# An eight-core encoder block: a fixed program with barriers against a list-scheduled one over pooled buffers

## The chip, the cores and the metric

The kernel runs on all eight cores of one Trainium2 chip, as two dies of four cores. Each core computes four whole sequences and shares nothing with the others. The metric is the device time of the slowest core, in microseconds (us).

Executions come in two states. In the slow one, the cores of one die (sometimes of both) show a lower mean granted TensorE clock, and the time is some per cent longer. Every comparison below is between fast executions, unless it says otherwise. "Excess" below means time in which TensorE was not doing columns at its full pace; how it is counted is told with the result.

## The reference, cut to what matters

One layer of an encoder block, on x of 32 x 2048 x 1024, memory of 32 x 256 x 1024:

```python
h = rms_norm(x, norm1_g)
proj = h @ w_in                       # 1024 -> 9728
y_dil = dilated_mixture_attention(...)   # 8 heads of 64, three (window, dilation): (128,1) (512,4) (2048,16)
y_ret = bidirectional_retention(...)     # 4 heads, forward and backward scan, per-head norm, silu gate
y_mem = memory_cross_attention(...)      # 4 heads of 128 into 256 memory tokens
gates = sigmoid(gate_p).reshape(b, s, 3, d)
merged = gates[:,:,0]*(y_dil @ w_branch_dil) + gates[:,:,1]*(y_ret @ w_branch_ret) + gates[:,:,2]*(y_mem @ w_branch_mem)
x = x + merged @ w_out
h2 = rms_norm(x, norm2_g)
x = x + conv_glu_ffn(h2, ...)            # 1024 -> 2 x 2816, conv of width 3, gelu * gate, -> 1024
```

In dilated attention the queries and keys have a norm per head, the scores get a position bias and a band mask, and the three dilations are merged by their softmax denominators.

## The kernel before

It is an in-order program. Each operation names keys that it reads and writes, each engine gets its operations in program order, and a barrier stands after the first norm, retention, memory attention, dilated attention and the output projection. PSUM banks go round by number, and scratch buffers are fixed.

```python
    def barrier(self, engines=("tensor", "vector", "scalar", "sync")):
        lasts = set(self.last[e] for e in engines if self.last[e] is not None)
        lasts |= set(v for k, v in self.last_dma.items() if isinstance(k, str) and k.startswith("xa"))
        for e in engines:
            self.bar[e] |= lasts
    # ... (cut)
        def bank():
            i = cnt["bank"] % 8
            cnt["bank"] += 1
            return ps[i], "ps%d" % i
    # ... (cut)
        def wload(src_ap, ncols, view=None):            # f32 in DRAM, cast to bf16 by the GpSimd DMA, every sequence
            s = nxt("w", 3)
            dst = wbuf[s][:, 0:8 * ncols].rearrange("p (k n) -> p k n", k=8)
            pairs = src_ap if isinstance(src_ap, list) else [(src_ap, view)]
            for sa, vw in pairs:
                P.op("gpsimd", lambda e, sa=sa, vw=vw: e.dma_start(out=dst if vw is None else vw(dst), in_=sa),
                     writes=["wbuf%d" % s], dma="wbuf%d" % s)
            return dst, "wbuf%d" % s
```

Dilated attention is twelve units: four pairs of heads by three dilations. For a unit, `prep` makes projections and head norms, `attn` makes scores, exponentials, the product with the position weights, and the product with the values. The program interleaves the attention of one unit with the projections of the next, by hand:

```python
            for u, (c, g) in enumerate(cgs):
                other = None
                if u + 1 < len(cgs):
                    c2, g2 = cgs[u + 1]
                    w_, wk_c = prep_begin(c2, g2, (u + 1) % 2)
                    other = prep_gen(c2, g2, (u + 1) % 2, w_, wk_c)
                # ... (cut)
                    interleave([attn_gen(c, g, u % 2)] + ([other] if other is not None else []))
            # ... (cut)
            P.barrier()
```

## Time and profile before

| | before |
|---|---|
| median of the first 6 runs | 7391.37 us |
| fast runs | 7197.74 to 7277.08 us, most of them under 7216 |
| slow runs | up to 7952.08 us |
| one sequence in the profiled run | 1791 us (1876 to 3667) |
| DMA | 357.63 MB in 470,679 packets |

The profiled run of before was a fast one (7205.49 us). The lines of the profile that matter are in the prediction. To read the stage windows there: the length of a window less the time that its matmuls need at full pace is what a better order could win.

### The profile page before, as it was taken

To read this page: it belongs to the slowest core of one execution; us is meant where nothing else is said; L and a number is where in the kernel's file an instruction comes from. 1 tells how busy PE (TensorE), PEld (TensorE's weight loads), DVE (VectorE), ACT (ScalarE), POOL (GpSimd) and SP (SyncE) were. 2 spreads that over 40 slices of the span, in tenths; PEclk is the share of its full clock that TensorE was granted. 3 is DMA by queue.
4 is the path that set the end of the run, shared out by engine and by line. 5 is a ranking of instruction groups with operands and counts; after the bars stand their busy time and mean duration, and the time that the engine had idled before them with its cause. 6 is when DMAs were issued, how large, how long until landed. Compare 5 with 4: busy or idle time off the path is not lost.

```text
span 7203.9 us, 101543 instructions; the slowest of 8 cores (7167.4 to 7203.9 us)
## 1 busy us (share of the span) xinstructions
PE 5903.6 (82%) x34768; PEld 2937.8 (41%) x34768; DVE 3232.9 (45%) x4627; ACT 2848.7 (40%) x5072; POOL 350.9 (5%) x401
## 2 busy tenths in 40 slices
PE   6478889899647888989964788898996478889898
PEld 3134544344323554444432345444443234544444
DVE  4335544561343554456143355445614335544561
ACT  4466632220346663232034666322203466632330
POOL 0000010000000001000000000100000000010000
PEclk9598889999859888999975988899997598889999
DMA  3111241435211114143521112424352111242424
GB/s 79 22 15 19 26 47 36 101 42 111 71 25 17 19 21 53 36 101 41 117 77 15 16 19 26 48 41 96 42 115 80 15 15 19 26 48 46 94 39 113
DMA packets 470679, 357.63 MB, mean 50 GB/s; under 512 B 259616, under 2 KB 405408, under 8 KB 470176
## 3 DMA queue, kind: packets, MB, share of 16 engines
q0 software_dynamic: 403792, 178.41, 20.7%
q1 hardware_dynamic: 66384, 172.72, 7.5%
q8 instruction: 290, 4.75, 0.3%
q14 instruction: 213, 1.74, 0.1%
HBM read 462.36 MB, written 67.11 MB: 73 GB/s over the span
## 4 chain that ended last, share of the span: by engine, by line
PE 72%; DVE 9%; ACT 8%; DMA 6%; issue 5%; DVEq 0%; SPq 0%; ACTq 0%; POOLq 0%
PE ps L415 29%; PE ps L727 10%; PE ps L1091 7%; PE ps L760 5%; PE ps L990 5%; PE ps L869 2%; PE ps L648 2%; PE ps L496 2%; PE ps L836 1%; PE ps L736 1%; DMA out<-arena 1%; DMA wbuf<-w_out 1%; PE ps L1026 1%; DMA arena<-w_in 1%; PE ps L841 1%
## 5 line engine op out<-in xcount | busy, mean ns | idle before, releaser
L415 PE MATMUL ps<-hT,wbuf 128*128 128x512 bf16 x6656 | 1454.3, 382 | 19.6 <-DVE arena L1043 6.4
L415 PEld LDWEIGHTS ps<-hT,wbuf 128*128 128x128 bf16 x6656 | 654.7, 98 | 817.5 <-issue 43.6
L727 PE MATMUL ps<-hT,wbuf 128*128 128x512 bf16 x3072 | 784.3, 402 | 31.6 <-DVE arena L741 13.1
L415 PE MATMUL ps<-hT,arena 128*128 128x512 bf16 x3072 | 732.9, 382 | 67.4 <-DMA arena<-w_in 67.4
L760 PE MATMUL ps<-wbuf,hT 128*128 128x128 bf16 x6144 | 406.9, 229 | 133.9 <-DVE arena L741 133.9
L415 PEld LDWEIGHTS ps<-hT,arena 128*128 128x128 bf16 x3072 | 301.7, 98 | 434.9 <-issue 76.9
L760 PEld LDWEIGHTS ps<-wbuf,hT 128*128 128x128 bf16 x6144 | 393.4, 124 | 138.9 <-issue 136.0
L727 PEld LDWEIGHTS ps<-hT,wbuf 128*128 128x128 bf16 x3072 | 289.3, 102 | 379.8 <-issue 125.1
L853 DVE TENSOR_TENSOR arena<-arena 128x512 bf16<-128x512 bf16 (+2 forms) x672 | 238.8, 357 | 360.0 <-ACT arena L850 295.0
L990 PE MATMUL ps<-arena,wbuf 128*128 128x512 bf16 x1536 | 396.7, 381 | 0.0
L1063 ACT ACTIVATE arena<-arena 128x2048 f32<-128x2048 f32 x88 | 168.2, 1912 | 547.1 <-DVE arena L1061 547.1
L850 ACT ACTIVATE arena<-ps 128x512 bf16<-128x512 f32 (+2 forms) x672 | 325.6, 490 | 100.4 <-PE ps L841 42.8
L985 ACT ACTIVATE t_1<-ps 128x512 f32<-128x512 f32 x256 | 152.9, 597 | 504.7 <-PE ps L415 481.9
L1066 DVE TENSOR_TENSOR arena<-arena,ps 128x512 bf16<-128x512 f32 x352 | 242.2, 688 | 230.5 <-PE ps L415 154.2
L1091 PE MATMUL ps<-wbuf,arena 128*128 128x512 bf16 x1408 | 313.4, 386 | 22.7 <-DVE arena L1066 22.7
L730 ACT ACTIVATE tball<-ps 128x512 bf16<-128x512 f32 x384 | 229.4, 597 | 250.0 <-PE ps L727 244.2
L1053 ACT COPY arena<-ps 128x512 f32<-128x512 f32 x352 | 205.2, 583 | 308.1 <-PE ps L415 307.5
L741 DVE SCALAR_TENSOR_TENSOR arena<-ps,par,t_0 128x512 bf16<-128x512 f32 x192 | 190.8, 994 | 295.8 <-PE ps L727 149.4
L1091 PE MATMUL ps<-arena 128*128 128x512 bf16 x1408 | 307.0, 380 | 9.6 <-DVE t_0 L1100 6.8
L869 PE MATMUL ps<-arena 128*128 128x128 bf16 x2048 | 247.0, 234 | 80.1 <-DVE arena L853 29.9
L386 ACT ACTIVATE xs<-arena 128x1024 bf16<-128x1024 f32 x48 | 50.7, 1057 | 641.6 <-DMA arena<-x 575.3
L575 PE MATMUL ps<-tball,arena 128*128 128x128 bf16 x256 | 73.2, 286 | 256.3 <-DVE tball L566 256.3
(206 smaller groups left out, 8135.2 us busy)
## 6 DMA issues: line engine op xcount, KB each, us to landing
arena<-x SPq DMA_DIRECT2D x96, 512.0 KB, 6.1
wbuf<-w_ffn_in POOLq DMA_DIRECT2D x88, 512.0 KB, 6.2
wbuf<-w_in POOLq DMA_DIRECT2D x144, 256.0 KB, 4.5
arena<-w_in POOLq DMA_DIRECT2D x96, 256.0 KB, 4.6
wbuf<-w_in POOLq DMA_DIRECT2D x16, 1024.0 KB, 14.4
xt<-x SPq DMA_DIRECT2D x32, 512.0 KB, 4.5
out<-xt SPq DMA_DIRECT2D x32, 512.0 KB, 5.5
out<-arena SPq DMA_DIRECT2D x32, 512.0 KB, 5.2
```

The source lines that it names most:

```text
L415: P.op("tensor", lambda e, kc=kc: e.matmul(bk[:, 0:n], lhsT=w[:, kc, coff:coff + 128], rhs=rhsT[:, kc, t0:t0 + n], start=(kc == 0), stop=( ...
L727: P.op("tensor", lambda e, kc=kc: e.matmul(bk[:, 0:512], lhsT=w[:, kc, coff:coff + 128], rhs=hT[:, kc, tt * 512:(tt + 1) * 512], start=(kc ...
L730: P.op("scalar", lambda e: e.activation(out=sq[:], in_=bk[:, 0:512], func=AF.Square), reads=[bkey], writes=[sqk])
L741: P.op("vector", lambda e: e.scalar_tensor_tensor(out=outv, in0=bk[:, 0:512].rearrange("p (i c) -> p c i", c=r), scalar=par[:, gcol:gcol + 1],
L760: P.op("tensor", lambda e, kc=kc, li=li, t0=t0: e.matmul(vb[:, li * 128:(li + 1) * 128], lhsT=hT[:, kc, t0:t0 + r * 127 + 1:r], rhs=w[:, k ...
L850: P.op("scalar", lambda e, lo=lo, hi=hi: e.activation(out=praw[:, lo:hi], in_=bs[:, lo:hi], func=AF.Exp, scale=0.125), reads=[bsk], writes ...
L853: P.op(meng, lambda e, lo=lo, hi=hi: e.tensor_tensor(out=pT[:, lo:hi], in0=praw[:, lo:hi], in1=Ets[st_][hh][:, lo:hi], op=ALU.mult), reads ...
L869: P.op("tensor", lambda e, oc=oc, m=m, pcx=pcx, ix=ix, n=len(tl): e.matmul(bn[:, oc], lhsT=dv[:, cl * ntile + m, vsl], rhs=pT[:, pcx:pcx + ...
L990: P.op("tensor", lambda e, kc=kc, bp=bp, bi=bi, oc=oc, yb=yb, tsl=tsl: e.matmul(bp[:, 0:512], lhsT=wbr[bi][0][:, kc, oc * 128:(oc + 1) * 1 ...
L1053: P.op("scalar", lambda e, bu=bu, tt=tt: e.copy(out=ubuf[:, 1 + tt * 512:1 + (tt + 1) * 512], in_=bu[:, 0:512]), reads=[buk], writes=["ubuf"])
L1066: P.op("vector", lambda e, bg=bg, tt=tt, j=j: e.tensor_tensor(out=yT[:, j, tt * 512:(tt + 1) * 512], in0=cbuf[:, tt * 512:(tt + 1) * 512], ...
L1091: P.op("tensor", lambda e, bk=bks[tl][0], j=j, t=t: e.matmul(bk[:, 0:512], lhsT=yT[:, j, t * 128:(t + 1) * 128], rhs=w[:, j - j0, 0:512], ...
```

## The change

The intent is to let stages overlap. The whole program is written down as a graph, without barriers; buffers are taken from pools; and a list scheduler, run when the kernel is built, fixes the order on each engine from a cost per operation. Besides that: the feed-forward part works on half a sequence, so that it can begin earlier; the f32 weights are cast once and kept in DRAM as bf16 copies; the mean of retention's head norm is folded into centred value weights; Sigmoid becomes Tanh, Silu is built from Exp and Ln; row norms take their reciprocal roots on GpSimd.

The files are nearly wholly rewritten, so the diff is cut to its core (cuts are marked by dots; the remarks behind # are added here).

```diff
-    def barrier(self, engines=("tensor", "vector", "scalar", "sync")):
-        lasts = set(self.last[e] for e in engines if self.last[e] is not None)
-        ...
+class Pool:
+    def __init__(self, name, aps, reserve, psum=False):
+        self.name, self.aps, self.reserve, self.psum = name, aps, reserve, psum
+        ...
+    def mm(self, out, lhsT, rhs, start=True, stop=True, skip=False):
+        n = elems(proto(rhs))
+        c = max(n / 2.4 + 2.5, 26)
+        ...
+    def schedule(self):
+        ...
+        def fits(i):                                   # may operation i take the buffers it needs now?
+            ...
+                old = tls[0].seq == p.oldest
+                if not old and k - len(tls) < p.reserve:
+                    return p
+                for tl in tls:
+                    if tl.cap and not old and p.held.get(tl.cap[0], 0) >= tl.cap[1]:
+                        return p
+        ...
+                while future[e] and future[e][0][0] <= free[e]:
+                    r, i = heapq.heappop(future[e])
+                    heapq.heappush(avail[e], (ops[i]["prio"], i))      # of the ready ones, program order wins
-        ps = [ctx.enter_context(nc.psum_tensor("ps%d" % i, [128, 512], F32)) for i in range(8)]
+        psp = P.pool("ps", [... 8 banks ...], psum_reserve, psum=True)   # reserve 2
+        fp = P.pool("F", bufs("fb", 6, [128, 512], F32), 3)
+        bp = P.pool("B", bufs("bb", 12, [128, 512], BF16), 4)
+        wp = P.pool("W", bufs("wb", 10, [128, 8, 128], BF16), 3)
+        def load(dst, src, cache, key, sem, after=None):
+            if key in cached:
+                P.dma("sync", dst, cache, sem, ...)                    # bf16 copy
+            else:
+                P.dma("gpsimd", dst, src, sem, ...)                    # f32, cast
+                    P.dma("sync", cache, dst, ...)                     # write the copy
+                    cached.add(key)
+        def phase_d():
+            ...
+            dil_prep(0, 0, 0)
+            for u, (c, g) in enumerate(units):
+                dil_attn(c, g, u % 2)
+                if g == 2:
+                    dil_tail(c)
+                if u + 1 < len(units):
+                    dil_prep(units[u + 1][0], units[u + 1][1], (u + 1) % 2)
+        for b in range(nseq):
+            ret_pair(0)
+            ret_pair(1)
+            phase_m(b)
+            phase_d()
+            gates(0)
+            load_wout()
+            out_proj(b, 0)
+            gates(1)
+            out_proj(b, 1)
+            ffn_in(0)
+            ffn_out(b, 0)
+            ffn_in(1)
+            mark = len(P.ops)
+            ffn_out(b, 1)
+            if b + 1 < nseq:
+                P.shift = mark - len(P.ops)                            # next norm at the last FFN out's priority
+                phase_a(b + 1)
+                P.shift = 0
```

The attention of a unit is in the new kernel:

```python
            def score(tiles):
                bs = [new(psp), new(psp)]                              # one PSUM bank for each head of the pair
                # ... 64-row score matmuls of both heads, alternately
                for hh in range(2):
                    raw, p = new(bp)[:, 0:o], new(bp)[:, 0:o]
                    P.act(raw, bs[hh][:, 0:o], AF.Exp, scale=0.125)
                    # ... P.tt(p, raw, E, ALU.mult): product with exp(-slope * distance), zero outside the band
```

## The prediction

> **What bounds the kernel now.** I read in this order: the times and the cores (all eight cores lie between 7167.4 and 7203.9 us, granted clock 0.886 to 0.890, so the profile is an undisturbed one and no core stands out); the page; then one sequence cut into its stages; then what ended TensorE's waits. The page first:
>
> ```profile
> PE 5903.6 (82%) x34768; PEld 2937.8 (41%) x34768; DVE 3232.9 (45%) x4627; ACT 2848.7 (40%) x5072; POOL 350.9 (5%) x401
> ...
> PE   6478889899647888989964788898996478889898
> ...
> PEclk9598889999859888999975988899997598889999
> ```
>
> Each core does four sequences, one after the other; the pattern of ten slices repeats four times. TensorE is the busiest engine, VectorE and ScalarE are under half. In every sequence there is a hole where PE is 4 to 7 tenths busy and its clock falls to 5 to 7 tenths. The stage windows of the second sequence (columns: window, length, busy PE, PEld, DVE, ACT, POOL, then granted clock, DMA share, GB/s):
>
> ```profile
> 1876.00:2123.00 247.00, 162.88 (x928) 78.95 (x928) 93.77 (x193) 100.89 (x206) 2.62 (x3) 0.71 0.08 13
> 2123.00:2252.00 129.00, 79.50 (x308) 31.21 (x308) 28.84 (x42) 74.51 (x134) 6.99 (x8) 0.84 0.20 25
> 2252.00:2708.00 456.00, 388.79 (x3299) 231.17 (x3299) 237.25 (x409) 291.12 (x519) 25.97 (x30) 0.89 0.20 22
> 2708.00:2762.00 54.00, 47.04 (x382) 28.15 (x381) 34.26 (x63) 30.76 (x60) 0.74 (x1) 0.78 0.13 21
> 2762.00:3026.00 264.00, 248.93 (x1143) 112.40 (x1144) 113.33 (x162) 64.09 (x102) 21.85 (x25) 0.96 0.27 29
> 3026.00:3134.00 108.00, 70.93 (x395) 32.87 (x392) 53.49 (x69) 28.23 (x66) 5.60 (x6) 0.92 0.73 182
> 3134.00:3445.00 311.00, 305.36 (x1408) 137.99 (x1408) 193.95 (x155) 92.66 (x111) 17.43 (x20) 0.99 0.30 41
> 3445.00:3600.00 155.00, 154.84 (x704) 69.45 (x704) 18.57 (x27) 0.00 (x0) 5.20 (x6) 0.98 0.56 132
> 3600.00:3667.00 67.00, 16.37 (x130) 12.54 (x130) 33.72 (x37) 27.52 (x65) 0.00 (x0) 0.53 0.49 167
> ```
>
> They are: retention, memory attention, dilated attention (two windows), gates, output projection with its norm, FFN in, FFN out, and the first norm of the next sequence. Only FFN in and out are full (1408 matmuls in 311 us). Dilated attention, the longest, is bound by nothing in full: PE 436 us busy of 510, by modelled ends, ACT 322.
>
> How much of "busy" is work? The timeline inside FFN in gives the pace:
>
> ```profile
> 3199.72 10.52 PE L415 MATMUL ps<-hT,wbuf 128*128 128x512 bf16 x48
> ```
>
> Less one latency (380 ns), 47 steps take 10.14 us: **215.7 ns for a 512-column matmul**, 0.421 ns a column, at clock 0.99. In dilated attention 32 matmuls of 128 columns take 1.95 us, less 0.23 for the last: 55.5 ns each, 0.434 a column. So PE's real work can be counted in columns. What ends PE's waits, over the whole run:
>
> ```profile
> PE ps L575 <- DVE tball L566: 256.3, 32, 10.1
> PE ps L399 <- DVE xs L391: 211.0, 63, 35.0
> PE ps L760 <- DVE arena L741: 133.9, 12, 11.5
> PE ps L399 <- DVE tball L391: 93.3, 64, 5.8
> ...
> PE ps L415 <- DMA arena<-w_in: 67.4, 4, 18.7
> ...
> PE ps L1026 <- DMA wbuf<-w_out: 42.6, 8, 8.9
> ```
>
> These are chains at the start or inside of a stage (retention's per-head norm, the norms before transposes, the change from one attention unit to the next) with no other stage's work to put in, and weight loads asked for only after a barrier. The kernel is TensorE work plus these holes and cold clock.
>
> **What the Trainium skill says.** (1) "TensorE: Matmul & The Clock Gate", Part 1: the array's clock is halved after an idle window of about 3.4 us and comes back after a busy one. The trace agrees: 0.53 and 0.71 in the windows with PE idle, 0.99 in FFN in. (2) The same page and part: with three cores of a die dense, the die is held at 13/16 of the clock. This profile does not show it: all eight cores have 0.99 in FFN in. But four of the six runs of before took 7374.86 to 7594.88 us against 7197.74, which may be this. (3) Same page, "Back-to-back issue gap": 215.7 ns is the isolated figure for 512 columns, and a sustained 131 ns is given too. The trace has 215.7 and never 131, so I use 215.7. (4) "DMA: Bandwidth & Descriptors", "Issuing engines are not separate DMA queues": queues of all issuers share the same 16 DMA engines, so moving loads from GpSimd to SyncE buys issue time, not bandwidth.
>
> **The change part by part.**
>
> *TensorE's work hardly changes.* Columns of a sequence, after: input projection 76 chunks of 128 outputs plus 2 for keys projected twice, each 8 x 2048 = 16384: 1,277,952; FFN in 44 x 16384 = 720,896; FFN out 360,448; branch projections 196,608; output 131,072; attention scores and values (31 tiles, 28 and 16 per head, 8 heads, twice) 153,600; memory keys and values 16,384, its attention 49,152; head norms 58,368; retention 57,344; transposes 34,816. Sum 3,056,640. Before it is about 12,000 more (the mean matmul of retention, now folded into centred weights, and padded edge tiles): 0.4%. About 0.41 M of them are in 128-column matmuls. So 2.65 M x 0.421 + 0.41 M x 0.434 = 1116 + 178 = **1294 us a sequence**, 5176 us for four. A sequence of before takes 1791 us (1876 to 3667), so 497 us of each is hole and cold clock, which I split by the same count: retention 247 - 125 = 122; memory 129 - 60 = 69; dilated 510 - 341 = 169; gates 264 - 249 = 15; output 108 - 63 = 45; FFN in 7; FFN out 3; first norm 67 - 7 = 60. The sum is 490. This is all that overlap can win.
>
> *No barriers, eight PSUM banks and all scratch in pools, order by a list scheduler.* Memory attention and the first dilated unit can start in retention's chains; out-projection norms of one half lie beside the gates of the other; FFN in on half 0 needs only the first tile of half 1; the next sequence's norm (7 us of PE) goes into the last FFN out. I expect left over per sequence: retention and memory 25 of 191, dilated 30 of 169 (below), gates and output 15 of 60, FFN 10, norm 5 of 60: **85 us**.
>
> *Other engines.* ACT in dilated attention, after, by the durations of before: 96 head norms x (597 + 682 + 630) = 183 us, 48 value copies x 584 = 28, 160 exponentials x about 560 = 90, tails 30, rest 17: **348 us against 341 of PE**. The durations overlap a little (an unrelated activation starts 0.53 us after one that lasts 0.63), so ACT occupies some 310. VectorE: 96 x 0.99 + 160 x 0.41 + 80 x 0.95 + 20 = 257. Near balance, hence the 30 us. Whole sequence: ACT about 655, DVE about 770 (FFN in 195, gates 110), both far under 1294. The reciprocal roots of the row norms go to GpSimd, and Sigmoid becomes Tanh[...]; before has only 15 table loads of 1283 ns, so that is 19 us at most.
>
> *Weights.* Before reads 89 MB of f32 weights a sequence, with 405,408 of 470,679 packets under 2 KB. After, sequence 1 reads f32 with a cast by GpSimd, and writes bf16 copies; the others read bf16 in 2 KB rows by SyncE: 196 tiles of 256 KB and 48 of 128 KB (gates and FFN weights are loaded twice, once per half) plus 8 MB = 66 MB, with some 43 MB of activations about 80 GB/s over 1380 us. FFN in of half 0 is densest: 11.5 + 5.8 MB in 155 us, 112 GB/s; before reached 182 GB/s at 0.73 DMA share and 265 at the start, so it is hidden. In sequence 1 that window must read 34.6 MB f32 and write 17 MB; FFN out of before took 0.56 share for 155 us for 132 GB/s (20 MB on chip, twice that in f32). By that ratio loads are about 0.5 and the writes 0.3 to 0.5 of the DMA time: at the limit, with the GpSimd issue in series. I add **80 us** once.
>
> *Ends.* Before needs 67 us until its first dense stretch. After: **60**, and 15 at the end.
>
> Sum: 4 x (1294 + 85) + 80 + 60 + 15 = **5671 us** for a fast execution; I round to 5650.
>
> **The rivals.** *ACT takes PE's place in attention.* The scheduler reckons a 512-column activation at 512 ns of occupancy; the trace has 597 to 682. A fixed order built on short times makes in-order PE wait at each miss. For: the 348 against 341. Against: the 0.53 us spacing. If ACT sets this stage at its full durations plus 10%, it lasts 385, not 371, and queues add more: 5750 to 5900. *Loads become the wait.* For: gate and FFN weights twice, one in-order SyncE queue where one load that waits for a buffer holds those behind it, and loads were waited for before (67.4 and 42.6 us). Against: 10 weight buffers of 256 KB, 7 us of PE each. If true, 5800 to 6000. *The clock.* A denser PE may spend more time in a slower clock: 5176 / 0.81 = 6390 with no gap at all, were the whole die held throughout. Against: 0.99 in dense FFN on eight cores. *Better than I think.* Scores now alternate the two 64-row halves of the array, head by head; if such pairs run together, half of 76,800 columns x 0.434 = 17 us a sequence go, and if the leftovers are halved too the sum is 5430.
>
> **Range and chances.** Fast executions: 5450 to 5850. Over the median of several, slow ones (2.5 to 5.5% on before) pull up, so I put the figure at 5700 and the range at 5400 to 6100. Even the clock rival leaves it faster than 7391 by over 10%: faster by over 2% 0.97, within 2% 0.02, slower 0.01.
>
> **What would show it.** Right: PE's slices at 9 nearly throughout, no dips of the clock but at the start; about the same matmul columns; span less 5176 is about 500 us, with holes mostly in sequence 1 and in attention; PE's waits there ended by ACT or by DVE behind ACT. ACT and DVE totals stay near 2600 and 3100. Wrong: waits on DMA in sequences 2 to 4 (loads); granted clock near 0.81 in dense stretches of a fast run (clock); a sequence time of over 1450 us with ACT near 90% in attention (ACT).

## The result, and the profile after

The change gave a median of **6160.61 us** (10 runs, 6047.86 to 6496.33), beside a median of 7379.80 us of 20 runs of before on the same chips. Its fast runs were 6047.86 to 6056.47 us, and the profiled one 6060.83. The ratio of fast runs, after over before, is **0.838** (95%: 0.834 to 0.842). A ratio is the mean time of one kernel's fast runs over that of the other's of the same rounds, so it is not quite the ratio of the medians quoted here.

So it is faster, as predicted, and by much, but not by as much as predicted: the fast runs lie 383 us above the worked-out 5671 and above the 5450 to 5850 given for fast executions, and the median lies above the range. Six of the ten runs were slow ones; in each, one die kept about the fast time (its cores took 6004 to 6087 us) while the other had a clock of 0.87 to 0.94. That is why the median is 107 us above the fast runs.

The page of after, to be held against the lines of before in the prediction:

```profile
span 6059.3 us, 109733 instructions; the slowest of 8 cores (6024.9 to 6059.3 us)
...
PE 5608.4 (93%) x35792; PEld 2869.8 (47%) x35792; DVE 3131.9 (52%) x4645; ACT 2601.1 (43%) x4575; POOL 323.9 (5%) x1057
...
PE   6889899989998999999998898999999898999999
...
PEclk9988899999998889999999888999999998999999
...
DMA packets 240025, 488.63 MB, mean 81 GB/s; under 512 B 26608, under 2 KB 54768, under 8 KB 238192
```

The hole in every sequence is gone: no slice is under 8 but the first. A shallow dip to 8, with the clock at 8, comes back four times. On the slowest core the records of the granted clock have 553 us at half clock, where those of before have 1639. The second sequence in its stages (same columns as in the prediction; the stages overlap at their edges, so the windows are where most of a stage lies): retention; memory attention; dilated attention; gates and output; feed-forward and the next norm.

```profile
1625.00:1775.00 150.00, 145.48 (x1492) 91.58 (x1490) 94.20 (x168) 67.00 (x120) 23.63 (x75) 0.98 0.19 56
1775.00:1890.00 115.00, 87.48 (x394) 33.89 (x393) 30.27 (x45) 75.56 (x139) 0.00 (x0) 0.94 0.11 30
1890.00:2311.00 421.00, 382.12 (x3136) 215.73 (x3135) 238.26 (x425) 304.86 (x554) 0.00 (x0) 0.87 0.08 23
2311.00:2640.00 329.00, 317.96 (x1551) 146.11 (x1552) 165.03 (x236) 85.41 (x143) 9.81 (x28) 0.99 0.34 105
2640.00:3105.00 465.00, 461.30 (x2369) 226.65 (x2368) 247.88 (x278) 111.92 (x181) 23.99 (x115) 1.00 0.37 114
```

Their sum is 1480 us, against 1791 before. Most stages are near full; memory attention (87 busy of 115 us) is not, and the longest hole is dilated attention, 421 us with the clock at 0.87. ACT is busy there 305 us, 72%: the sequence is over the 1450 us that the prediction named as a sign of its ACT rival, but ACT isn't near 90%. What ended TensorE's waits in the whole run (first columns: total us, times, longest), and below it in the dilated window alone:

```profile
PE ps L489 <- DVE bb L489: 129.4, 209, 2.0
PE ps L489 <- ACT fb L489: 113.2, 131, 3.0
PE ps L489 <- DVE fb L489: 90.4, 62, 32.5
...
PE ps L489 <- DVE bb L489: 30.4, 48, 1.5
PE ps L489 <- ACT fb L489: 6.0, 3, 2.0
```

No weight load stands among the waits. The largest entry, `DVE bb`, is a value matmul of attention that waits for VectorE's product with the position weights.

**The balance.** To see how much is left, I matched the 35,792 matmuls of the trace one to one with the program's order, so that each has its stage, and summed their columns: 12,227,264 (predicted 4 x 3,056,640 = 12,226,560). At the 0.4213 ns a column that the dense stretches show, that is 5151 us. What a stage takes from start to start of its matmuls, over its columns, is its excess; here for the second sequence (the third and fourth have 192 and 190 in all):

| us in the second sequence | predicted left over | measured excess |
|---|---|---|
| retention and memory attention | 25 | 61 (25 and 36) |
| dilated attention | 30 | **109** |
| gates and output | 15 | 17 |
| feed-forward | 10 | 6 |
| first norm | 5 | 0 |
| sum | 85 | **193** |

The first sequence has 108 us more than the others (50 of them in the feed-forward part, where the f32 weights are read and copies written, 28 in retention), and 33 us pass before the first matmul: 141, predicted 80 + 60. The later sequences have 191.8 us on average, so 4 x (191.8 - 85) = 427 us is what the prediction missed, less 25 for columns that cost slightly less than reckoned and 15 for an end that was not found. The rest of this document is about the 109.

**Inside dilated attention.** The timeline of after while one residue class of dilation 4, every fourth position, passes (start, length, engine, operation, times, and in brackets the idle time before it and what ended it):

```profile
1947.83 1.11 ACT L489 ACTIVATE bb<-ps 128x448 bf16<-128x448 f32 x2 [2.19 <-DVE bb L489]
1947.88 1.09 PE L489 MATMUL ps<-bb,arena 128*128 128x192 bf16 x4 [1.41 <-DVE bb L489]
1948.55 1.22 DVE L489 TENSOR_TENSOR bb<-bb,arena 128x256 bf16<-128x256 bf16 x4 [0.24 <-PE ps L489]
...
1949.35 0.53 PE L489 MATMUL ps<-bb,arena 128*128 128x256 bf16 x2 [0.37 <-DVE bb L489]
...
1949.99 2.08 DVE L489 TENSOR_TENSOR arena<-arena,ps 128x512 f32<-128x512 f32 x2 [0.22 <-PE ps L489]
...
1951.94 1.25 DVE L489 TENSOR_TENSOR bb<-bb,arena 128x192 bf16<-128x192 bf16 x4
...
1952.77 0.53 PE L489 MATMUL ps<-bb,arena 128*128 128x192 bf16 x2 [1.42 <-DVE bb L489]
```

The pattern repeats after 4.89 us or so (1947.88 to 1952.77). In that time VectorE is busy 1.22 + 2.08 + 1.25 = 4.55 us, 93%, with eight products and two sums. The class has 3584 columns, 1.51 us at full pace, and TensorE has no projection among them: here the attention of a unit runs alone. ScalarE's exponentials, which empty the score banks, wait for VectorE too (2.19 us idle, ended by `DVE bb`). With the matmuls matched by unit, the 109 us lie so: attention of dilation 4 has 35, of dilation 1 27, of dilation 16 only 1.5, and the projections between them 45.

The clock is part of it. The records of the granted clock in this trace know only 1.000 and 0.500, in stretches that are multiples of 3.4 us; each attention of dilation 1 falls into half clock for 10 us and each of dilation 4 for 14, that of dilation 16 never. One attention each of dilation 1, 4 and 16 (columns as before; the clock is the first number after the five engines):

```profile
2012.00:2029.00 17.00, 15.27 (x92) 6.59 (x90) 9.02 (x24) 12.56 (x24) 0.00 (x0) 0.70 0.07 17
2049.00:2070.00 21.00, 15.57 (x93) 6.49 (x91) 14.61 (x39) 10.40 (x20) 0.00 (x0) 0.67 0.05 14
2090.00:2099.00 9.00, 8.35 (x93) 5.24 (x92) 6.82 (x15) 6.14 (x12) 0.00 (x0) 1.00 0.09 31
```

The stretches go on into the projections. Columns begun at half clock make 230 us in the whole run, so at most 230 us are lost to it, and at most 46 us a sequence in dilated attention. But half clock comes after TensorE has waited: it may be a result rather than a cause.

So four theories stood for the experiments:

- **VectorE's chain**: score, exponential, product, value matmul; the product is the pace while attention runs alone.
- **The clock**: once at half speed, attention stays slow by itself.
- **ACT**: the rival of the prediction; head norms and exponentials.
- **PSUM hoarding**: score tiles take the banks, so the projections that should fill TensorE's gaps find none.

### The profile page after: what moved, and what is told of

Read it like the earlier page. It is cut to its first block, busy times and chain, and to the rows that moved or that the text cites. A ratio compares the mean times of both kernels' runs of the same rounds, so it can differ in the third digit from the quotient of the medians.

```text
span 6059.3 us, 109733 instructions; the slowest of 8 cores (6024.9 to 6059.3 us)
## 1 busy us (share of the span) xinstructions
PE 5608.4 (93%) x35792; PEld 2869.8 (47%) x35792; DVE 3131.9 (52%) x4645; ACT 2601.1 (43%) x4575; POOL 323.9 (5%) x1057
## 4 chain that ended last, share of the span: by engine, by line
PE 79%; ACT 7%; DVE 6%; issue 5%; DMA 1%; POOL 1%; DVEq 0%; ACTq 0%; SPq 0%; POOLq 0%
PE ps L489 79%; ACT fb L489 4%; ACT bb L489 2%; DVE bb L489 2%; DVE xb L489 1%; DVE arena L489 1%; POOL sc L489 1%; DVE fb L489 1%; DVE sb L489 1%; DMA bb<-w_branch 0%; DMA xb<-x 0%; ACT xb L489 0%; DVEq L487 0%; DVE hT L489 0%; ACTq L487 0%
## 5 line engine op out<-in xcount | busy, mean ns | idle before, releaser
L489 PE MATMUL ps<-hT,wb 128*128 128x512 bf16 (+2 forms) x14016 | 3193.4, 377 | 102.4 <-ACT fb L489 78.7
L489 PEld LDWEIGHTS ps<-hT,wb 128*128 128x128 bf16 x14016 | 1373.4, 99 | 1561.2 <-issue 220.7
L489 PE MATMUL ps<-arena 128*128 128x512 bf16 (+4 forms) x6656 | 1133.5, 327 | 25.6 <-DVE arena L489 14.9
L489 ACT ACTIVATE bb<-ps 128x512 bf16<-128x512 f32 (+1 forms) x1296 | 725.8, 583 | 389.7 <-DVE bb L489 201.3
L489 PEld LDWEIGHTS ps<-arena 128*128 128x128 bf16 (+2 forms) x6656 | 497.7, 98 | 606.2 <-issue 144.0
L489 PE MATMUL ps<-wb,hT 128*128 128x128 bf16 x9216 | 563.8, 221 | 9.1 <-DVE hT L489 7.4
L489 PEld LDWEIGHTS ps<-wb,hT 128*128 128x128 bf16 x9216 | 546.8, 113 | 34.5 <-issue 13.4
L489 PE MATMUL ps<-bb,arena 128*128 128x128 bf16 (+3 forms) x2240 | 439.4, 292 | 130.7 <-DVE bb L489 126.9
L489 DVE SCALAR_TENSOR_TENSOR xb<-xb,par 128x1024 f32<-128x1024 f32 x352 | 452.1, 1284 | 37.0 <-DVE xb L489 1.8
L489 ACT ACTIVATE fb<-fb 128x512 f32<-128x512 f32 (+2 forms) x724 | 439.0, 624 | 34.9 <-DVE fb L489 14.6
```

Of the source, the lines that this page charges most:

```text
L489: ins = getattr(e, o["m"])(*[real(x) for x in a], **{k: real(v) for k, v in kw.items()})
```

## The experiments

Each runs beside the kernel before on the same chip. Fast runs of before in the same calls were 7201 to 7215 us, but for one of 7260.56, so fast times can be compared to some tenths of a per cent; "against after" below means against 6054 us (the mean of 6048 to 6061). "Plan" is the end that the scheduler reckoned for its own order; it is 5771 us for after. The edits are cut and simplified to their core.

### Does hoarding keep the projections out?

The cap that the program has, but does not use, set to two banks for score tiles.

```diff
-                bs = [new(psp), new(psp)]
+                bs = [new(psp, ("sc", 2)), new(psp, ("sc", 2))]
```

> One change: the score tiles of dilated attention may hold at most 2 of the 8 PSUM banks at a time; same instructions, another order. Theory (PSUM): score matmuls, first in priority, take every free bank up to the reserve, so no projection of the next unit can start and attention runs alone, paced by ScalarE and VectorE, with TensorE a third busy and its clock halved. Then projections of the next unit now stand between the score pairs, the stage falls from about 450 us towards 380 to 400 a sequence, half-clock time in it falls by more than half, and the run is 200 to 300 us shorter than after (ratio to it 0.95 to 0.967). Rival (ACT): ScalarE's 250-odd us of the stage set it; then the order does not matter and the time is within 1% of after. Rival (clock): the halved clock is a cost by itself, whatever the order; then half-clock time stays and so does the time.

Measured: 5989.90 us (one fast run, correct), 64 shorter. Dilated attention, second sequence:

```profile
1870.00:2273.00 403.00, 383.51 (x3158) 214.55 (x3159) 242.13 (x432) 303.84 (x568) 0.00 (x0) 0.96 0.08 24
```

The clock there goes from 0.87 to 0.96 and the excess from 109 to 83, with 18 of it at half clock. The waits for the product (`DVE bb`) fall from 129 us to 51 in the run. So hoarding had a part, but a third of the least that this theory named. The new order also has a price: it changes 1794 times between matmuls of 64 and of 128 rows, where after does so 1130 times. At the 0.1 us each that the runs below show, that is up to 66 us (an estimate), so less hoarding may have won about twice what the time shows.

### Is it the clock?

Six matmuls of 512 columns, whose result is overwritten, before each pair of score tiles of dilations 4 and 16.

```diff
+                for hh in range(2 if g else 0):
+                    for _ in range(3):
+                        P.mm(bs[hh], ident, hT[:, 0, 0:512])
                 for cl, m in tiles:
```

> Added work, same result: before each score pair of dilations 4 and 16, six 512-column matmuls that are overwritten (1152 more matmuls, about 249 us of TensorE at full clock in all, put where it waits). Theory (PSUM): attention alone is paced by ScalarE and VectorE, so the half clock costs only the matmuls that begin in it, at most 46 us a sequence in this stage; time between 100 us shorter and 60 us longer than after, with the half-clock time of the stage cut by over half. Rival (clock): the half clock is the main cost; then 150 to 200 us shorter. Rival (TensorE is the bound in the stage): up to 249 us longer.

Measured: 6158.15 us (one fast run, correct), some 100 longer, which is outside the range expected from the PSUM theory. The columns of dilated attention rise from 334 to 396 us a sequence, the excess falls from 109 to between 72 and 78. So 62 us of added columns bring back some 34, most of it half clock (46 at most before, about 21 now).

The edit missed a part of its aim. Half clock comes at dilations 1 and 4, and the added matmuls stood at 4 and 16. At dilation 16 there was nothing to warm, and dilation 1 stayed as it was (excess 26, 14 of it at half clock). At dilation 4 no half clock was left, and there and in the projections behind it 32 us came back for 42 us of added columns. So keeping TensorE warm did not pay for itself where it was tried. That the clock follows from the waits is shown better by two runs below: without the product the clock comes back by itself, and in the run with scores over 128 rows the half clock in attention of dilation 4 falls from 11 or 12 to between 5 and 7 us a sequence, while the excess there stays at 35.

### Is it ACT?

The head norms of dilated attention without their Ln (wrong, relative error 0.066): 96 activations a sequence less.

```diff
-            P.act(r, b2, AF.Ln, bias=eps_c)
-            P.act(r, r, AF.Exp, scale=-0.5)
+            P.act(r, b2, AF.Exp, scale=-0.5)        # in dilated attention only
```

> Wrong result on purpose: the head norms of the dilated queries and keys leave out the logarithm, 384 activations of 690 ns, about 57 us of ScalarE occupancy a sequence, in the projection part of the stage. Rival (ACT, the one named in the prediction): the stage falls by 40 to 55 us a sequence, the run by 160 to 220 us. Theory (PSUM): the projections are bound by TensorE and attention has none of these activations beside it, so within 40 us of after.

Measured: 6072.38 us in the one fast run; the undisturbed dies of two slow runs show 6050 to 6073. Nothing won: the profiled run was a slow one, and the sequences that its cores passed at their usual clock have an excess of 105 to 112. **ACT's head norms do not set the pace.** Its exponentials are still there in this run; they are in the next one too, which is much shorter, so the ACT rival of the prediction falls.

### Is it VectorE's product?

The exponential goes straight to the value matmul (wrong, relative error 0.128).

```diff
-                    raw, p = new(bp)[:, 0:o], new(bp)[:, 0:o]
-                    P.act(raw, bs[hh][:, 0:o], AF.Exp, scale=0.125)
-                    ... P.tt(p, raw, E, ALU.mult)
+                    p = new(bp)[:, 0:o]
+                    P.act(p, bs[hh][:, 0:o], AF.Exp, scale=0.125)
```

> Wrong result on purpose: attention leaves out the product of the exponentials with the position weights, about 57 us of VectorE a sequence, and with it one link of the chain score, exponential, product, value matmul. Theory (PSUM): this chain paces attention while nothing else runs on TensorE, so the stage falls by 30 to 50 us a sequence, the run by 120 to 200 us. Rival (ACT): ScalarE has the same work as before, so within 40 us of after.

Measured: 5819.81 us (one fast run; undisturbed dies of slow runs 5806 to 5822), **235 shorter**, more than the 120 to 200 expected. The window of dilated attention, on a core of the undisturbed die of the profiled run:

```profile
1840.00:2183.00 343.00, 331.89 (x2866) 193.93 (x2863) 163.05 (x183) 274.66 (x508) 0.00 (x0) 0.99 0.09 26
```

VectorE falls from 425 to 183 operations, and the clock comes back by itself, to 0.99, with no warming. The excess falls from 109 to about 50, with 2 to 9 at half clock; at dilation 4 it falls from 35 to 13, at dilation 1 from 27 to 9. The plan fell by 129 us only, so the chip won more than the scheduler reckoned; one thing that the scheduler does not know is the clock. The edit also takes one buffer less for each exponential, which was not tested apart from VectorE's time.

### Is it the strided writes of the head norms?

VectorE writes queries and keys at a stride of the dilation, and adds to strided sums. Here both are contiguous (wrong, relative error 0.113).

```diff
-                    if r == 1:
-                        out = dst[:, tt * 512:(tt + 1) * 512]
+                    out, inv = dst[:, tt * 512:(tt + 1) * 512], None
-                        view = accs[hh].rearrange("p (i c) -> p i c", c=r)[:, :, cl]
+                        view = accs[hh][:, cl * 512:cl * 512 + 512]
```

> Wrong result on purpose: in dilated attention VectorE writes queries and keys, and adds values to the sums, at contiguous places instead of places 4 or 16 apart; same number of instructions. Measured before in the changed kernel: 998 ns in place of some 690 for a norm product, 862 in place of 686 for a sum, about 45 us of VectorE a sequence; the scheduler, which reckons both alike, plans only 35 us less for the whole run (finer dependences). Theory now (VectorE): the run without the position product was 235 us shorter and the one without the logarithms not shorter, so VectorE and the chain through it pace the stage; then this run is 100 to 200 us shorter than after. Rival (order alone: the PSUM theory): about 35 us shorter, as planned.

Measured: 5990.18 us (one fast run), 64 shorter, between the two theories. The groups by form (busy us, mean ns of one), first after, then this kernel; all are 512 columns from PSUM:

```profile
L489 DVE SCALAR_TENSOR_TENSOR arena<-ps,par,fb 128x512 bf16<-128x512 f32 x384 | 379.4, 998 | 310.7 <-PE ps L489 164.4 <-ACT fb L489 145.9
L489 DVE TENSOR_TENSOR arena<-arena,ps 128x512 f32<-128x512 f32 x256 | 221.9, 885 | 27.3 <-PE ps L489 24.5
```

```profile
L489 DVE SCALAR_TENSOR_TENSOR arena<-ps,par,fb 128x512 bf16<-128x512 f32 x384 | 285.2, 750 | 429.9 <-ACT fb L489 249.8 <-PE ps L489 179.6
L489 DVE TENSOR_TENSOR arena<-arena,ps 128x512 f32<-128x512 f32 x256 | 172.8, 683 | 26.1 <-PE ps L489 23.6 <-issue 0.3
```

Strides cost 143 us of VectorE time in the run. The plan, which reckons both kernels alike, is 35 us shorter too, from finer dependences, so what the strides themselves cost at the end is some 29 to 64 us (an estimate), at most 16 us a sequence.

### Can the product be avoided in a correct kernel?

The position bias, a multiple of the distance, is added in PSUM by a matmul of the identity with a bias tile; the exponential then gives the weighted score.

```diff
-                P.act(Ets[s][hh], dist[:], AF.Exp, scale=-(2.0 ** (-(2 * c + hh + 1))) * r)
+                P.act(Ets[s][hh], dist[:], AF.Copy, scale=-8.0 * (2.0 ** (-(2 * c + hh + 1))) * r)
                     for hh in range(2):
                         P.mm(bs[hh][:, o:o + hi - lo], dk[...], dq[...], True, False)
+                    for hh in range(2):
+                        P.mm(bs[hh][:, o:o + hi - lo], ident, Ets[s][hh][:, e0:e0 + hi - lo], False, True)
```

> Correct result: the position weights are added to the scores in PSUM by a matmul of the identity with a bias tile (exact in bf16: whole multiples of powers of two), and VectorE's product goes. TensorE gets 307,200 columns more, 129 us, VectorE loses 640 products of 192 to 512 columns, about 230 us. Theory (VectorE paces the stage): the stage falls by 59 - 32 = about 27 us a sequence, the run by 80 to 140 us. Rival (TensorE is the bound in the stage): longer by up to 129 us.

Measured: 5995.96 and 5995.45 us, correct, 58 shorter. The columns grow by 307,200 (129 us at full pace, 32 a sequence), the excess in dilated attention falls from 109 to 65, and 4 of that are at half clock. It removes the wait, but pays in columns, and 65 is more than the 50 of the kernel without a product. Its order has 2490 changes between matmuls of 64 and of 128 rows, that of the kernel without a product 1340; the next kernels show what a change costs.

### Memory attention earlier, and the parts together

Memory attention before the second half of retention, with the cap:

```diff
             ret_pair(0)
-            ret_pair(1)
             phase_m(b)
+            ret_pair(1)
```

> The score cap of 2 banks, and memory attention put before the second half of retention in the order of priority, so that retention's projections can fill its waits. Memory attention takes 96 us of TensorE's time for 60 us of columns in the changed kernel, waiting for ScalarE. If that is want of other work: 20 to 30 us a sequence less than with the cap alone, 80 to 120 us in all, so about 5880. If its own chain with its six PSUM banks a unit keeps others out: within 30 us of the cap alone (5990).

Measured: 5942.49 and 5939.99 us, correct, some 50 shorter than the cap alone, between the two cases expected. The excess of memory attention falls from 36 to 26 a sequence and that of dilated attention from 84 to 72, while retention's rises from 25 to 28. So a small part of the 61 us of retention and memory was order.

Then all of it at once: the bias by TensorE, the cap, memory attention first, and a scheduler that is told the measured cost of strided VectorE operations (0.75 ns an element more).

> Correct result: position weights by TensorE, the score cap, memory attention before the second half of retention, and the scheduler told that VectorE's strided operations take 0.75 ns an element more. Its plan at full clock is 5669 us against 5846 for the changed kernel reckoned with the same costs. If VectorE's pace, PSUM hoarding and memory attention are together the cause of the 400 us that the prediction missed: 5720 to 5800, granted clock over 0.98. If they do not add: 5850 to 5950.

Measured: 6064.10 and 6056.99 us, correct: **no better than after**, where the cap, the bias and memory attention's place had given 64, 58 and some 50 (the told costs had not been run alone). The clock was 1.00 in dilated attention, yet the excess there 79 to 83. The timeline shows why (same columns as above; core 4):

```profile
1901.81 0.28 PE L496 MATMUL ps<-arena 64*128 64x256 bf16 x1
1902.03 0.28 PE L496 MATMUL ps<-arena,cb 128*128 128x256 bf16 x1
1902.24 0.28 PE L496 MATMUL ps<-arena 64*128 64x256 bf16 x1
1902.45 0.28 PE L496 MATMUL ps<-arena,cb 128*128 128x256 bf16 x1
```

A matmul of 256 columns needs 0.108 us, and none of these waits for anything, but they start 0.21 us apart. They alternate between 64 rows of the array (a score of one head) and 128 (a bias). In its trace a matmul of 128 rows after one of 64 begins about 104 ns late, 64 after 128 about 98 ns. This kernel's order has 3088 such changes, after has 1130, the bias kernel 2490.

The same kernel with the bias matmuls joined to one of up to 512 columns, ahead of the scores:

```diff
+                    if ntile == 1:
+                        P.mm(bs[hh].rearrange("p (k i) -> p k i", k=4), ident, E[:, 64:192].unsqueeze(1).to_broadcast([128, 4, 128]), True, False, skip=True)
+                    elif w_ == 512:
+                        P.mm(bs[hh].rearrange("p (k i) -> p k i", k=2), ident, E[:].unsqueeze(1).to_broadcast([128, 2, 256]), True, False, skip=True)
                     # ... (cut: else one bias matmul for each tile)
                     # ... then the 64-row scores, accumulating
```

> The kernel of e9_all with one thing changed: the bias matmuls of a score pair come first, up to 512 columns at once, then all its score matmuls, in place of bias and scores in turn. In the trace of e9_all a matmul of 128 rows that follows one of 64 rows, or the other way round, starts about 100 ns late (means of 97 to 105 ns over thousands of such pairs, none waiting), and there are some 2450 such changes in all, 60 us a sequence. Theory (changes of row count are a cost of TensorE's own): 1500 or more fewer changes, so 100 to 190 us shorter than e9_all, 5870 to 5950. Rival (the 100 ns belong to the waits and not to the change): within 40 us of e9_all's 6057.

Measured: 5923.45 and 5926.06 us, correct. 136 us shorter for 1152 changes fewer, some 118 ns each. Here is the missing cost.

### The same cost in the changed kernel

After, with its scores taken over all 128 rows (wrong: the two heads are mixed, relative error 0.113). The columns, the plan and the other engines' work stay as they were; the changes of rows fall from 1130 to 626.

```diff
-                        P.mm(bs[hh][:, o:o + hi - lo], dk[hp[hh], ...], dq[hp[hh], ...])
+                        P.mm(bs[hh][:, o:o + hi - lo], dk[:, ...], dq[:, ...])
```

> Wrong result on purpose: the score matmuls of dilated attention in the changed kernel take all 128 rows (both heads) instead of 64; the order is the same, the plan is the same 5771 us. The changes between 64-row and 128-row matmuls go from 1130 to 626. Theory (a change costs TensorE about 100 ns where it is not waiting anyway): 10 to 60 us shorter, less than 504 x 0.1 = 50 us on the whole, since most of the changes stand in stretches that wait for VectorE, and pairs of heads no longer run side by side (6 us a sequence lost). Rival (changes are a main part of the miss in the changed kernel as well): over 80 us shorter.

Measured: 6004.26, 6003.50 and 6006.44 us, 50 shorter for 504 changes fewer. The excess in dilated attention is 94 to 98. It gives up that the scores of two heads run side by side (in after, two of 192 columns pass in 0.09 us), and wins all the same. But half clock in the stage fell too, from 43 to 22 us a sequence on average, so these 50 us are no clean price of a change.

### Was the order built on wrong times?

The cap and memory attention first, with the truer costs of strided operations.

```diff
         c = n * 1.042 / sp
+        if strided([in0, out] + others):
+            c += 0.75 * n
```

> The kernel of e7_mfirst, scheduled with 0.75 ns an element more for VectorE's strided operations, as measured; only the order changes. Its plan goes from 5640 to 5724 us because the costs are told, not because the order is worse. Theory (a fixed order built on short times makes TensorE wait, a rival of the prediction): 20 to 60 us shorter than e7_mfirst's 5941. Rival (finer mixing adds changes between 64-row and 128-row matmuls at 100 ns each): within 20 us, or longer.

Measured: 6012.59, 6006.43 and 6064.17 us, correct; 65 or more longer than the same kernel without (5941). Truer times of strided operations made the order worse; why stays open. ScalarE's times, which the prediction named as told too short, were left as they were, so that rival of a fixed order built on short times is tested only in part.

### Where did the gain come from?

Barriers back in the changed kernel, at the starts of retention, memory attention, dilated attention, gates and feed-forward (for compute; loads still run ahead):

```diff
+    def barrier(self, cell):
+        b = self.mset(cell, 0.0)
+        for i in self.since:
+            if i != b:
+                self.ops[b]["deps"][i] = 0
+        self.bar, self.since = b, []
```

> The changed kernel with barriers again where the kernel before had them (before retention, memory attention, dilated attention, gates and FFN in): compute operations wait for all compute of the stage before; loads do not. Theory of the prediction: overlap between stages is a part of the gain. The scheduler plans 188 us more, and ends and starts of stages at half clock add to it: 190 to 300 us longer than after (6250 to 6350), leaving over two thirds of the gain to the order inside the stages. Rival (overlap between stages is the gain): near 7000.

Measured: 6326.35 and 6341.53 us, 0.879 of before (0.877 to 0.881), correct. Of the 1150 us between the fast runs of before and after, barriers would take back only 280. Excess a sequence: first norm 17 to 22, retention 28 to 31, memory 60 to 64, dilated 107 to 118, gates and output 29 to 31, feed-forward 7 to 10. In sum that is some 264, where the prediction's split has 490 for before and after has 192; retention alone had 122 before. **Most of the gain is won inside the stages**, not by the overlap of stages. How much of it is order, and how much the rewritten operations, no run here separates. Loads still ran ahead in this run, so what late loads cost before is not in the 280. The trace of before also has 2160 changes between 64 and 128 rows, after 1130: up to 100 us of the gain, by the same price (an estimate).

No bf16 copies in DRAM: every load reads f32 through the casting queue.

```diff
-                if nseq > 1 or key[0] in ("f1", "br", "in", "out"):
+                if False:
```

> The changed kernel without bf16 copies: GpSimd loads f32 weights with a cast in every sequence, twice for gates and FFN in. The first sequence of the changed kernel does just that and shows an excess of 57 us in the FFN against 6 in the others, and 21 against 16 in gates and output. Theory (loads were hidden in most of before, and copies matter in FFN in of half 0 alone): 50 us a sequence in three sequences, 100 to 250 us longer than after. Rival (copies are a large part of the gain): over 400 us longer.

Measured: 6167.37 and 6160.19 us, 0.856 of before (0.854 to 0.858), correct: the copies are worth 110 us. The excess of the feed-forward part rises from 6 to between 34 and 39 a sequence, that of dilated attention from 109 to 120.

### A better version

The joined bias without the truer costs, with the cap, then without it.

> The kernel of e10_group without the costs told to the scheduler, 1936 changes of row count as there. Telling the costs made the kernel of e7_mfirst 66 us longer (e12_calib). If the order made with short costs is the better one here too: 5860 to 5910 against 5925. If not: 5925 to 5980.

> The kernel of e14_best without the cap on score banks: with no product on VectorE the score banks are emptied by ScalarE alone. If hoarding of PSUM is then no longer a limit: within 30 us of e14_best, perhaps shorter for 194 fewer changes of row count. If hoarding still keeps projections out: 40 us longer or more, with half-clock time in the stage.

Measured: with the cap 5926.92 and 5926.01 us, the same as with the truer costs, so they neither harm nor help here, and I had expected better. Without the cap 5866.79, 5867.20 and 5865.88 us, correct: **0.811 of before** (0.804 to 0.818), 187 us under after. The verdict on it is marked unclear, presumably because one fast run of before was 7260.56; the kernel's own three runs agree within 1.4 us. Its page and its dilated attention:

```profile
PE 5608.0 (96%) x36752; PEld 2912.0 (50%) x36752; DVE 2855.1 (49%) x3685; ACT 2562.9 (44%) x4563; POOL 321.5 (5%) x1057
...
PEclk9999999999999999999999999999999999999999
...
1835.00:2221.00 386.00, 383.11 (x3354) 224.47 (x3353) 170.03 (x190) 298.48 (x550) 0.00 (x0) 1.00 0.09 25
```

In dilated attention no half clock is left (7 to 14 us of columns a sequence begin in it elsewhere), and a sequence takes 1425 us. The cap, which gave 64 us in after, **costs 60** here, where at most 30 either way or 40 longer was expected without it; some 20 of it may be its 194 more changes of rows (an estimate). So hoarding hurt together with the product, which held the exponentials up, and not by itself.

## Why the prediction was right or wrong

**Right: the direction, and the mechanism in part.** TensorE's columns are those counted, to 0.01%. Holes were filled, not work removed. But the prediction put this down to the overlap of stages, and the run with barriers gives only 280 of 1150 us back: most holes were filled inside their stage. Gates and output, feed-forward and first norm have 17, 6 and 0 us left, predicted 15, 10 and 5. No load ends a wait of TensorE. The first sequence and the start cost 141 us, predicted 140, which is luck: they are 108 and 33, predicted 80 and 60. ACT and VectorE totals are 2601 and 3132 us, predicted "near 2600 and 3100". The scores of two heads in the two halves of the array do run side by side where they stand next to each other (two of 192 columns start 3 ns apart). The suspicion about the slow runs fits: in the two traces of slow runs (without the logarithms, without the product) the slow dies have stretches at 0.8125, which is 13/16.

**Wrong: the step "I expect left over per sequence: retention and memory 25 of 191, dilated 30 of 169".** They are 61 and 109. That is 115 us a sequence; the other stages were 7 better, which leaves 108 in the second sequence and 106.8 on average. Four times that is 427; with 1 for first sequence and start, less 25 for cheaper columns and 15 for an end that was not found, it is the 388 between 5671 and the profiled 6059. Of the 139 us that dilated attention was to win (169 - 30), 60 came.

- The 30 rested on a balance over the stage: ACT 348 and VectorE 257 beside 341 of TensorE. As totals these are roughly right (305 and 238 in the window), though the products were counted as 160 a sequence and are 240. But the stage is not one mixture. The scheduler's priority is the order of the program, attention of one unit, then projections of the next, and where attention runs alone VectorE is 93% busy and TensorE a third. An average over the stage hid it. This is the rule about busy shares, one level deeper than stages.
- The rival that I named, ACT, is false: 96 activations fewer won nothing (its short times in the scheduler were not tried). VectorE, which I reckoned at 257 us beside 341 and made no rival, sets the pace through the product with the position weights: 235 us less without it.
- The clock rival was set up wrongly. I asked if dense work lowers the clock. In the fast runs it does not; what came was half clock at dilations 1 and 4, after waits, up to 46 us a sequence in this stage.
- A cost was not in the sum at all: the change between matmuls of 64 and 128 rows, some 0.1 us each, 1130 times, so up to 113 us of the run (an estimate from that price and count; a change hidden in a wait costs nothing). "TensorEngine Tiling (Array Packing)" in the Trainium skill, section "Key Properties", says that a change of tiling mode drains TensorE. I had not drawn on it. I counted only what the two halves win, as the "better than I think" rival.
- A small reading was wrong: before has 24 table loads on ScalarE, not 15, and after has 20, one of them before the Gelu of each sequence, so 4 loads of 1.28 us fewer in all.

In dilated attention the 109 us a sequence are then, as an estimate: up to 46 half clock, 37 of waits seen in its window (30.4 + 6.0, and 0.9 in two smaller lines), and 13 for 126 changes of rows (504 over four), 96 together. They overlap and influence each other, so this is no sum: cap, no product, no strides, bias by TensorE and 128-row scores won 64, 235, 64, 58 and 50 us singly, and such gains did not add up.

**Wrong in its median.** For slow runs I allowed some 50 us over a fast figure; six of ten runs were slow, by 102 to 442 us, which put the median 107 over the fast runs. The fast time and the 50 allowed make 6104, at the upper bound of 6100; the slow runs put it well past.

**Open.** What the 36 us of memory attention consist of beyond the 10 that its place won; what is left of the 34 us in the best version's dilated attention, of which its 279 changes of rows a sequence would make 28 (an estimate); why truer costs gave a worse order with the product and made no difference without it; and why a die falls into the slow state in some runs and not in others.

## What to carry to other kernels

When stages are merged, look at what runs beside what in the new order, not at the totals of a stage: a part that runs alone has its own bound, and here it was the engine that was lightly loaded on average. Before giving an elementwise step on a chain of matmuls to VectorE, see if TensorE can do it in PSUM, with few and wide matmuls, and keep matmuls of different row counts in runs. Try improvements together as well as singly: three that each won 50 to 64 us won nothing together (with truer costs told beside them), and one of them, the cap, turned into a loss once its reason was gone.

## What the Trainium skill lacked or had wrong

- "TensorEngine Tiling (Array Packing)", "Key Properties", has the drain at a change of tiling mode, but no figure, and "TensorE: Matmul & The Clock Gate", Part 3, does not mention it. The runs show some 97 to 105 ns per change in the traces, and 118 ns from the times of two kernels that differ by 1152 changes.
- "TensorE: Matmul & The Clock Gate", "Back-to-back issue gap", gives a sustained 131 ns for 512 columns. The traces have 215.7 ns in the densest stretches, which this section calls the isolated figure, while Part 1 of the same page measures it back to back.
- The same page, Part 1, has a die with three dense cores held at 13/16 while the load lasts. Fast runs do not show it: in the best version TensorE is 96% busy, and all eight cores have a mean clock of 0.987 to 0.989 over 5865 us. Slow runs fit it: the two traces of slow runs have stretches at exactly 0.8125 = 13/16 (2189 of 6140 us and 4514 of 6695 us on the slowest cores; none on the undisturbed die), and in one run without a trace a die had a mean of 0.816 to 0.820, with the other at 0.987 to 0.990. So it comes in some executions of a kernel and not in others.
- "VectorE: DVE Perf Modes", "Mode 1× (REGULAR) — the baseline", says that odd strides and PSUM operands work at one result a cycle. A penalty for strides is named elsewhere in the skill ("SBUF — State Buffer", "Door 1: The DMA port swizzle"), but no page has a figure for one on VectorE. A sum of 512 f32 columns took 885 ns on strided sums and 683 on contiguous ones.
